# One more pair of k-tiles by seven products in two output projections of an encoder block

## The chip, the cores and the metric

The kernel runs on one core of one Trainium2 chip. The metric is the device time of one execution in microseconds (us). The engines of a core run side by side: PE (TensorE) multiplies matrices, DVE (VectorE) and ACT (ScalarE) work on elements, POOL (GpSimd) does little here, and SP (SyncE) issues the transfers from and to device memory. Each engine takes its instructions in a fixed order, and an instruction waits until what it reads has been written and the buffer it writes is free.

## The reference

One layer of an encoder on 256 tokens with 2048 channels, all in float32:

```python
x = x + 0.5 * swiglu(rms_norm(x, ffn1_norm), ffn1_w_gate, ffn1_w_up, ffn1_w_down)
h = rms_norm(x, mix_norm)
u, q, k, v, g, a_lr = jnp.split(h @ w_in, IN_SPLITS, axis=-1)
x = x + jnp.concatenate([pool_mixer(u, ...), gla_mixer(q, k, v, g, a_lr, ...)], axis=-1) @ w_out
x = x + mem_cross_attention(rms_norm(x, xattn_norm), rms_norm(mem, mem_norm), w_q, w_kv, w_o)
x = x + 0.5 * swiglu(rms_norm(x, ffn2_norm), ffn2_w_gate, ffn2_w_up, ffn2_w_down)
out = rms_norm(x, final_norm)
```

Two products matter below: the mixer's output product with `w_out` (2048 x 2048) and the attention's with `w_o` (2048 x 2048), which ends `mem_cross_attention`.

## The kernel before, in words

**Products in two parts.** Every operand is split into a high and a low part (`split`, `split_weights`), and a product of 128 x 128 by 128 x 512 is made of three instructions on PE: high by high, high by low weight, low by high weight (`products`, L356). ACT copies the high part of the weights (`wh`, L273), DVE subtracts it from the weights to get the low part (`wl`, L274).

**The stream.** A weight matrix comes in loads of 1 MB (two k-tiles of 128 rows by 1024 columns, buffer `raw`, three of them). The class `Stream` walks through all loads in order; it splits a load up to `AHEAD = 2` places before PE uses it, and asks for the load three places on as soon as a split is done. The buffers `wh` and `wl` are there three times. `op(f, n)` puts a piece of work n loads later into the order. `among_weights` and `in_turn` fix where such work stands between the splits on DVE and ACT.

**Seven products.** A load has two k-tiles and two halves of 512 columns, and there are two halves of 128 tokens: a 2 x 2 by 2 x 2 block product, 8 products of three instructions each, 24 on PE. For a pair of k-tiles that a block lists among its `sevens`, the block product is made of 7 products (21 instructions, function `seven`, L480) in Winograd's way. For that DVE adds blocks of the weights into a tile `T` (L457: one add of 128 x 1024, two of 128 x 512), ACT and DVE split the three raw blocks (`xh`, `xl`, 128 x 1536) and the four sums (`wh` L460, `wl` L461, 128 x 2048): `split_seven`. The left operand needs sums too, once for each pair: class `Sums`, with four adds on DVE (L418 to L430) and the splits of their results into the tile `ye` and back into the activations. `room` says how many pairs' sums share the first tile.

**A block.** `block_s` computes one half of the columns (1024) of an output: 8 loads in a given order of the pairs 0 to 7. Its plain products are summed in one pair of PSUM tiles; P1, P5, P6 and P7 of the seven-product pairs go to a second pair of tiles. PSUM has room for four such tiles. After the last pair of `sevens`, `combine` joins the parts (L547 to L552) and `merge` adds them to the residual x (L742); after the last load `join` adds the plain sums (L730).

**Output products.** `into_x` runs two blocks (column halves) of `block_s` for each output product. It fetches x from device memory for each half (`fetch_x`), and one load after a half ends it turns the new x (`fold`, L763), which takes two PSUM tiles, and computes its squares (L772) and its scaled parts (L242, L234). An object of `IntoX` holds the pairs, when their sums are made, the orders and the `sevens` of both halves. `OUTPUT` is the one for mixer and attention: pairs 0 and 4 by 7 products in both halves, in the 5th and 7th place of the first half and the 3rd and 5th of the second. Its sums are made by `OUTPUT.make_sums`, for the mixer 1 and 4 loads after the stream comes to it, for the attention 0 and 4.

**Where the left operands come from.** For the mixer, k-tiles 0 to 7 (pairs 0 to 3) come from the pool group and k-tiles 8 to 15 (pairs 4 to 7) from the four heads of the linear attention. For the attention, head h gives the pairs 2h and 2h + 1; the values of the last two heads (`values`, L1330) are computed while the first loads of `w_o` are being used.

**The order** of the instructions on each engine is made by a scheduler when the program is built, within what `among_weights` and its like fix. It moves single products of PE forward or back to fill waits that it expects.

## Time and profile before

| | us |
|---|---|
| median of three runs | 2085.72 |
| lowest and highest run | 2085.29, 2086.19 |
| span of the profiled execution, first to last instruction | 2085.1 |
| PE busy in it | 2071.5 |
| DVE busy | 1820.8 |
| ACT busy | 1137.5 |

The profile is that of one execution. Its span leaves out some 0.6 us before the first and after the last instruction that a run's time has. Its lines name the source line, the engine, the operation and the tiles (output, then what it is made from). A timeline's row gives the start and the duration in us, and in square brackets the idle time before it with what ended it. On PE a product's duration (0.39 us) is longer than the distance to the next one, because products overlap: PE's pace is read from starts. The same holds in a small way for DVE, whose rows overlap the next by some 0.09 us. In the chain of what ended last, each piece has its start, its length and the number of instructions.

The mixer's output product runs from about 914 to 1002 us, the attention's from about 1287 to 1380 us.

### The profile page before, as it was taken

The numbers are of one execution on the slowest core, as the hardware profiler recorded it, in microseconds if no ns is written. First come the engines' busy times: TensorE is split into PE (matmuls) and PEld (weight loads), VectorE is DVE, ScalarE is ACT, GpSimd is POOL, SyncE is SP. The second block draws the span as 40 slices with busy tenths as digits, with TensorE's granted clock in tenths as the row PEclk, the third lists the DMA queues.
The fourth block names the chain that finished last, engine by engine and source line by source line (L and its number), as shares of the span: only waits on it lengthen the run. The fifth ranks groups of instructions, "written<-read, shape, count | busy, mean of one in ns | idle before, by whom it ended". The sixth has DMA issues, their size and how long they took to land.

```text
span 2085.1 us, 24238 instructions
## 1 busy us (share of the span) xinstructions
PE 2071.5 (99%) x9660; PEld 1727.2 (83%) x9660; DVE 1820.8 (87%) x1670; ACT 1137.5 (55%) x1128; POOL 13.1 (1%) x41
## 2 busy tenths in 40 slices
PE   9999999999999999999999999999999999999998
PEld 7888888888888888888888888888888888888886
DVE  6999899989998677579789777879998999989997
ACT  7555455554555545455755444556554556545554
POOL 0000000000000000000000000000000000000001
PEclk9999999999999999999999999999999999999999
DMA  7656766566656755457655455666576665676664
GB/s 263 201 189 235 242 220 204 187 229 232 225 197 234 238 177 182 162 182 269 225 186 188 162 182 179 205 223 203 181 242 213 236 209 190 223 241 223 204 223 159
DMA packets 131321, 435.94 MB, mean 209 GB/s; under 512 B 9860, under 2 KB 13544, under 8 KB 130824
## 3 DMA queue, kind: packets, MB, share of 16 engines
q1 hardware_dynamic: 131176, 434.38, 61.4%
q8 instruction: 76, 1.25, 0.2%
q14 instruction: 37, 0.30, 0.0%
q10 hardware_dynamic: 32, 0.01, 0.0%
HBM read 417.58 MB, written 16.78 MB: 208 GB/s over the span
## 4 chain that ended last, share of the span: by engine, by line
PE 96%; DVE 2%; issue 1%; ACT 0%; DMA 0%; SPq 0%; DVEq 0%
PE pt L356 57%; PE pt L480 26%; PE pa L341 6%; PE pb L356 2%; PE ph L752 1%; PE pl L1291 1%; PE pv L1330 1%; PE px L763 1%; DVE wl L461 0%; DVE T L457 0%; DVE xl L274 0%; DVE wl L274 0%; DMA x<-in_x 0%; PE pp L984 0%; PE pe L356 0%
## 5 line engine op out<-in xcount | busy, mean ns | idle before, releaser
L274 DVE TENSOR_TENSOR wl<-raw,wh 128x2048 fp32r<-128x2048 f32 (+2 forms) x264 | 591.4, 2247 | 131.1 <-ACT wh L273 130.4
L356 PE MATMUL pt<-wh,xs 128*128 128x512 f32 x2128 | 681.8, 390 | 0.0
L273 ACT CAST wh<-raw 128x2048 fp32r<-128x2048 f32 (+2 forms) x264 | 495.4, 1880 | 284.4 <-PE pt L356 128.1
L356 PEld LDWEIGHTS pt<-wh,xs 128*128 128x128 f32 x2128 | 398.2, 188 | 81.7 <-ACT wh L273 0.4
L356 PE MATMUL pt<-wh,ys 128*128 128x512 f32 x1472 | 464.7, 390 | 0.0
L460 ACT CAST wh<-T 128x1024 fp32r<-128x1024 f32 x236 | 248.0, 1054 | 380.5 <-DVE T L457 370.0
L356 PE MATMUL pt<-wl,xs 128*128 128x512 f32 x1064 | 415.5, 391 | 0.0
L356 PEld LDWEIGHTS pt<-wh,ys 128*128 128x128 f32 x1472 | 275.9, 188 | 56.9
L356 PE MATMUL pt<-wl,ys 128*128 128x512 f32 x736 | 286.3, 389 | 0.0
L461 DVE TENSOR_TENSOR wl<-T,wh 128x2048 fp32r<-128x2048 f32 x118 | 269.5, 2284 | 0.7
L356 PEld LDWEIGHTS pt<-wl,xs 128*128 128x128 f32 x1064 | 199.8, 188 | 41.1
L274 DVE TENSOR_TENSOR xl<-raw,xh 128x1536 fp32r<-128x1536 f32 x118 | 206.7, 1752 | 19.2 <-ACT xh L273 19.2
L273 ACT CAST xh<-raw 128x1536 fp32r<-128x1536 f32 x118 | 174.6, 1480 | 41.4 <-PE pt L480 29.2
L457 DVE TENSOR_TENSOR T<-T,raw 128x512 f32<-128x512 f32 x236 | 162.8, 690 | 6.2
L356 PEld LDWEIGHTS pt<-wl,ys 128*128 128x128 f32 x736 | 138.2, 188 | 28.6
L457 DVE TENSOR_TENSOR T<-raw 128x1024 f32<-128x1024 f32 x118 | 143.8, 1219 | 0.5
L480 PE MATMUL pt<-wh,xs 128*128 128x512 f32 x364 | 141.8, 389 | 0.0
L480 PE MATMUL pt<-xh,xs 128*128 128x512 f32 x364 | 136.6, 391 | 0.1
L341 PE MATMUL pa<-xs,wh 128*128 128x512 f32 x384 | 135.6, 397 | 0.0
L480 PE MATMUL pt<-wh,xe 128*128 128x512 f32 x320 | 124.5, 389 | 0.0
L341 PE MATMUL pa<-xs,wl 128*128 128x256 f32 x384 | 106.8, 282 | 0.0
L341 PEld LDWEIGHTS pa<-xs,wh 128*128 128x128 f32 x384 | 71.7, 188 | 16.4 <-issue 0.3
(244 smaller groups left out, 2215.6 us busy)
## 6 DMA issues: line engine op xcount, KB each, us to landing
raw<-in_ffn_w_down SPq DMA_DIRECT2D x88, 1024.0 KB, 5.5
raw<-in_ffn_w_up SPq DMA_DIRECT2D x80, 1024.0 KB, 5.0
raw<-in_ffn_w_gate SPq DMA_DIRECT2D x77, 1024.0 KB, 5.1
raw<-in_w_in SPq DMA_DIRECT2D x32, 1024.0 KB, 5.2
raw<-in_xattn_w_kv SPq DMA_DIRECT2D x32, 1024.0 KB, 5.0
raw<-in_w_out SPq DMA_DIRECT2D x16, 1024.0 KB, 5.6
raw<-in_xattn_w_q SPq DMA_DIRECT2D x16, 1024.0 KB, 5.6
raw<-in_xattn_w_o SPq DMA_DIRECT2D x16, 1024.0 KB, 5.9
```

The costliest lines, as they stand in the source:

```text
L273: in_turn("scalar", lambda: nc.scalar.copy(hi, src))
L274: in_turn("vector", lambda: nc.vector.tensor_tensor(out=lo, in0=src, in1=f32(hi), op=ALU.subtract))
L341: nc.tensor.matmul(o, w, x, start=k == 0 and i == 0, stop=last and i == 1)
L356: nc.tensor.matmul(ps, a, w, start=first and i == 0, stop=last and i == 2)
L457: in_turn("vector", lambda: nc.vector.tensor_tensor(out=o, in0=a, in1=b, op=ALU.add))
L460: in_turn("scalar", lambda: nc.scalar.copy(th[:, c], t[:, c]))
L461: in_turn("vector", lambda: nc.vector.tensor_tensor(out=tl, in0=t, in1=f32(th), op=ALU.subtract))
L480: nc.tensor.matmul(banks[n], x, w, start=n in fresh and j == 0, stop=n in ends and j == 2)
L752: nc.tensor.transpose(v[:, i, h * P : (h + 1) * P], g[:, h, i * P : (i + 1) * P], ident)
L763: nc.tensor.transpose(v[:, j, h * P : (h + 1) * P], x[:, h, j * P : (j + 1) * P], ident)
L1291: nc.tensor.matmul(ps[:, t, :M], ys[:, 4 * h + d, a, tok], xa["K", h][:, d, b, :], start=i == 0, stop=i == 11,)
L1330: nc.tensor.matmul(ps[:, d, :S], xa["V", h][:, m, a, col], xa["PT", h][:, m, b, :], start=i == 0, stop=i == 5,)
```

## The change

`OUTPUT` gets a third pair, number 2 (k-tiles 4 and 5), in both halves and so in both output products. The orders are new: in the first half the 7-product pairs 2, 0, 4 stand in places 4, 6 and 7; in the second half in places 2, 4 and 6. The sums of pair 2 are made first: for the mixer after 1, 3 and 4 loads, for the attention after 0, 2 and 4. Their tile `ye` has room for three pairs instead of two.

```diff
-        def __init__(self, pairs, after, orders, sevens, over=True):
-            self.sums = Sums("ye", ys, pairs, over, 2)
+        def __init__(self, pairs, after, orders, sevens, over=True, room=2):
+            self.sums = Sums("ye", ys, pairs, over, room)
             self.after, self.orders, self.sevens = after, orders, sevens
...
-    OUTPUT = IntoX((0, 4), (0, 4), ((1, 2, 3, 5, 0, 6, 4, 7), (1, 2, 0, 3, 4, 5, 6, 7)),
-                   ((0, 4), (0, 4)))
+    OUTPUT = IntoX((2, 0, 4), (0, 2, 4), ((1, 3, 5, 2, 6, 0, 4, 7), (1, 2, 3, 0, 5, 4, 6, 7)),
+                   ((2, 0, 4), (2, 0, 4)), room=3)
...
-    OUTPUT.make_sums((1, 4))
+    OUTPUT.make_sums((1, 3, 4))
```

## The prediction

> **What bounds the kernel now.** I read the page first, for the shares, then the busy time in stretches of the two blocks, then the chain in order of time, then the timelines of the matrix and the vector engine there.

> ```profile
> span 2085.1 us, 24238 instructions
> PE 2071.5 (99%) x9660; PEld 1727.2 (83%) x9660; DVE 1820.8 (87%) x1670; ACT 1137.5 (55%) x1128; POOL 13.1 (1%) x41
> PE 96%; DVE 2%; issue 1%; ACT 0%; DMA 0%; SPq 0%; DVEq 0%
> ```

> The matrix engine (PE) is busy throughout and is 96% of the chain that ends last. That says that a removed product is a gain, as long as nothing else is short. The vector engine (DVE), busy 87% over the whole span, is not 87% busy everywhere:

> ```profile
> core 0: us, PE busy (x) PEld busy (x) DVE busy (x) ACT busy (x) POOL busy (x), PEclk, DMA share, GB/s
> 936.40:958.40 22.00, 22.00 (x99) 18.22 (x98) 20.72 (x21) 11.69 (x10) 0.00 (x0) 1.00 0.67 223
> 958.40:980.30 21.90, 21.90 (x106) 18.39 (x105) 21.04 (x23) 13.75 (x22) 0.00 (x0) 1.00 0.78 261
> 980.30:1002.00 21.70, 21.70 (x97) 17.98 (x96) 17.83 (x12) 9.28 (x6) 0.00 (x0) 1.00 0.86 317
> 1314.90:1336.70 21.80, 21.80 (x98) 18.06 (x97) 20.68 (x21) 11.70 (x10) 0.00 (x0) 1.00 0.66 220
> 1336.70:1358.70 22.00, 22.00 (x107) 18.42 (x106) 21.13 (x23) 13.76 (x22) 0.00 (x0) 1.00 0.82 266
> ```

> These are the middle of the mixer's output product (936 to 980) and of the attention's (1315 to 1359). DVE idles 1.28 + 0.86 = 2.1 us in the first 44 us and 1.12 + 0.87 = 2.0 in the second. PE and DVE are balanced there, and the change adds work to DVE in just these blocks.

> **What it removes.** The pitch of a product comes from the chain in order of time (start, us, what):

> ```profile
> 969.43 1.75 PE px L763 x16
> 977.08 5.44 PE pt L480 x24
> 984.79 22.00 PE pt L356 x97
> ```

> 5.44 / 24 = 22.00 / 97 = 0.227 us. A load of the usual kind (call its place in a block "plain") takes 24 products, one with 7 products takes 21. One more pair in each of the four output blocks (two column halves, mixer and attention) removes 4 x 3 x 0.227 = 2.7 us. This is the whole gain that is to be had: 0.13%.

> **What it adds.** The vector engine's timeline in the mixer's block shows a plain load, a pair's sums and a 7-product load one after the other without idle time:

> ```profile
> 935.01 2.29 DVE L274 TENSOR_TENSOR wl<-raw,wh 128x2048 fp32r<-128x2048 f32 x1
> 937.22 0.68 DVE L418 TENSOR_TENSOR j<-ys 128x512 f32<-128x512 f32 x1
> ...
> 939.33 1.22 DVE L457 TENSOR_TENSOR T<-raw 128x1024 f32<-128x1024 f32 x1
> 940.47 0.55 DVE L280 TENSOR_TENSOR ye<-j,ye 128x384 fp32r<-128x384 f32 x1
> 940.93 1.41 DVE L457 TENSOR_TENSOR T<-T,raw 128x512 f32<-128x512 f32 x2
> 942.26 1.75 DVE L274 TENSOR_TENSOR xl<-raw,xh 128x1536 fp32r<-128x1536 f32 x1
> 943.93 2.28 DVE L461 TENSOR_TENSOR wl<-T,wh 128x2048 fp32r<-128x2048 f32 x1
> 946.13 2.28 DVE L274 TENSOR_TENSOR wl<-raw,wh 128x2048 fp32r<-128x2048 f32 x1
> ```

> By the starts: plain 2.20 us; 7 products 1.14 + 1.33 + 1.67 + 2.20 = 6.34; sums 2.11 + 0.46 = 2.57. So each block gets 6.34 - 2.20 = 4.14 us, and mixer and attention each one more set of sums: 4 x 4.14 + 2 x 2.57 = 21.7 us of DVE time. **Bounds:** all of it hidden gives 2085.1 - 2.7 on the span; all of it exposed gives 2085.1 + 19.0. A program of this kernel takes 0.6 us more than its span (median 2085.72 beside 2085.1), so 2083.0 to 2104.7.

> How much is exposed I work out by laying the changed order of DVE instructions, which the built kernel shows, end to end with these durations, and comparing with when PE comes to the weights. First block of the mixer: 7 products now stand in places 4, 6 and 7 of 8 (before: 5 and 7).

> ```profile
> 927.60 0.69 DVE L280 TENSOR_TENSOR ys<-t,ys 128x512 fp32r<-128x512 f32 x1 [0.74 <-ACT ys L279]
> ```

> ```profile
> 947.49 0.39 PE L480 MATMUL pt<-xl,ys 128*128 128x512 f32 x1
> ```

> Before, the xl of place 7 was ready at 943.93 and PE used it at 947.49: 3.56 us to spare. Now DVE reaches it later by 4.14 + 2.57, less about 0.6 of the idle 0.74 us above, which the new order closes: 6.1 us. PE comes 3 x 0.227 = 0.7 us earlier. **PE waits 6.1 + 0.7 - 3.6 = 3.2 us** at place 7, plus some 0.1 for wl right behind it. Behind the waiting product stand all later ones: PE works in order.

> From there DVE and PE start level, and the second block begins. Its 7-product places move from 3 and 5 to 2, 4 and 6, and the merging of the first block's parts still lies in between:

> ```profile
> 952.51 1.23 DVE L549 TENSOR_TENSOR sg<-pt,sg 128x1024 f32<-128x1024 f32 x1
> ...
> 957.07 0.69 DVE L552 TENSOR_TENSOR sg<-pt,sg 128x512 f32<-128x512 f32 x1
> 957.67 1.22 DVE L742 SCALAR_TENSOR_TENSOR x<-sg,x 128x1024 f32<-128x1024 f32 x1
> ...
> 960.54 1.22 DVE L730 SCALAR_TENSOR_TENSOR x<-pt,x 128x1024 f32<-128x1024 f32 x1
> ```

> Up to the wl of place 3, DVE has to do: wl of places 7 and 8 and of place 1 (3 x 2.20), one 7-product load (6.34), L548 and L552 (0.60 each, like the 957.07 to 957.67 above), L549 (1.2), two L742 (1.13 each, a row's 1.22 less the 0.09 by which it overlaps the next) and one more wl: 19.8 us. PE has 18 + 23 + 35 = 76 products to that point, 17.2 us. **It waits about 2.5 us.** From there to the wl of place 5: DVE T (1.14), two L730 (2.26), the rest of the load (5.20), wl (2.20) = 10.8, and 0.3 for a copy of ACT's that now stands behind its squares; PE 33 products and the 16 transposes, 7.5 + 1.75 = 9.2. **It waits about 1.8 us.** After place 6 DVE's slack of 980 to 1002 (3.9 us) takes over. Mixer: 3.3 + 2.5 + 1.8 and some 0.2 of hand-over = 7.8 us.

> Attention: the same orders, but its first 7-product load stands behind the values of the last two heads.

> ```profile
> 1307.45 0.59 ACT L279 CAST ys<-pv 128x512 fp32r<-128x512 f32 x1 [0.85 <-PE pv L1330]
> 1307.93 1.48 ACT L273 CAST xh<-raw 128x1536 fp32r<-128x1536 f32 x1
> 1309.32 2.00 ACT L460 CAST wh<-T 128x1024 fp32r<-128x1024 f32 x2
> ```

> ```profile
> 1307.41 7.51 PE pt L356 x33
> 1314.92 2.72 PE pt L480 x12
> ```

> PE reaches place 4 some 5.44 us before 1314.8, at 1309.3; the values end earlier too, at about 1304.8 by the changed order, so ACT's xh copy follows at 1305.3 and xl starts at 1306.7: in time. Then DVE: wl of place 4 ends at 1310.9, then sums 2.11, wl 2.20, a 7-product load with ye 6.80, sums 2.11, and T, ye and xl of place 7, 4.6: 1328.7. PE is there after 70 products, at 1325.2: 3.5 us. With the second block as above, 8.2 us.

> **Sum:** 7.8 + 8.2 - 2.7 = +13.3 us on the span of 2085.1, with the 0.6 around it **2099.0 us**, between the bounds and nearer to full exposure, because the idle time of DVE in these stretches is 2 us each.

> Hidden: ACT's extra copies (1.48 + 2.00 in the rows above against 1.9 in the row under (c), sums 0.8) fall on an engine that is busy 11.7 of 22 us; uncovered they would be 1.6 us per block. SP fetches x for the first block one load earlier; place 7's load is issued behind it.

> ```profile
> raw<-in_w_out SPq DMA_DIRECT2D x16, 1024.0 KB, 5.6
> ```

> It lands 5.6 us after its buffer is free (about 930), and DVE asks for it at 945; without that lead the wait would be a part of 5.6 us once per product.

> **Rivals.** (a) *DVE catches up.* Only the first blocks' waits are seen, 3.3 + 3.5 - 2.7 = +4.1 us: 2089.8. For it: DVE has idle time later. Against: that lies behind place 6, and the merges stand before it. (b) *Not slower: the lead is there.* The place is the wait for ACT ahead of the block:

> ```profile
> 911.08 2.29 DVE L274 TENSOR_TENSOR wl<-raw,wh 128x2048 fp32r<-128x2048 f32 x1 [3.31 <-ACT wh L273]
> ```

> If DVE could use these 3.3 us, place 7 would be in time; from a lead of 7 us more on, all is hidden and 2083.0 remains. Against: the wait is for buffers that PE frees, and no added instruction stands ahead of it. (c) *Held buffers.* In the second block the parts of places 2 and 4 are put off to after place 5, so their high weights keep two of three buffers, and places 3, 5 and 6 share one. A copy then starts only when PE leaves the place before:

> ```profile
> 977.12 1.92 ACT L273 CAST wh<-raw 128x2048 fp32r<-128x2048 f32 x1 [0.86 <-PE pt L356]
> ```

> Copy and subtraction take 1.9 + 2.2 = 4.1 us; 9 products and 16 transposes (3.8) cover the first, 24 put-off products (5.4) the second. I count nothing; where they add to DVE's delay, up to 4.1 per second block: 2107.2. (d) *The clock.* A wait of 3.2 us is longer than PE's longest so far:

> ```profile
> 10.21 0.63 PE L689 MATMUL px<-ident,x 128*128 128x128 f32 x4 [2.21 <-DMA x<-in_x]
> 10.00:12.00 2.00, 1.79 (x10) 1.61 (x11) 0.48 (x1) 0.57 (x2) 0.00 (x0) 1.00 1.05 411
> ```

> After 2.21 us the granted clock stayed at 1.00. If it fell to half after each wait at place 7, for as long as the wait, that would cost 2 x 1.6 = 3.2 us: 2102.2. [...]

> **How the numbers follow.** Forecast 0.66 (its own range 2094 to 2104); (a) 0.15; (b) 0.04; (c) 0.07; (d) 0.08. Left out at most 2 in 10: 2088.5 to 2104.5. What this kernel's measurement can tell from no change is about 0.2%, 4.2 us: faster is out of reach of the 2.7 us (0.01); the same holds for (b) and half of (a) (0.11); slower 0.88.

> **What would show it.** PE idle with DVE's xl (L274) as releaser at the seventh place of both first blocks, about 3 us; with wl at places 3 and 5 of the second blocks, 1.5 to 3 us; DVE without gaps from 925 to 990; L480 with 84 products more, L356 with 96 fewer. Wrong it is if PE has no gaps there, if ACT or a load is the releaser, or if the granted clock drops.

## The result and the profile after

The changed kernel takes 2099.49 us (median of 4 runs, 2098.82 to 2099.82), the one before 2085.95 beside it (4 runs, 2085.29 to 2088.73): a ratio of 1.0064, 95% interval 1.0052 to 1.0076, or 13.5 us more. The forecast was 2099.0.

From the page of the changed kernel, the lines of the span, of the engines and of the chain that ended last:

```profile
span 2096.7 us, 24269 instructions
PE 2076.0 (99%) x9648; PEld 1727.0 (82%) x9648; DVE 1841.0 (88%) x1700; ACT 1144.7 (55%) x1140; POOL 13.1 (1%) x41
PE 91%; DVE 6%; issue 2%; ACT 1%; DVEq 0%; POOL 0%; ACTq 0%; POOLq 0%
```

PE has its 12 products fewer and DVE 20.2 us more. In the chain DVE's share rises from 2% to 6%. The busy times of the stretches from before show where (columns as there):

```profile
core 0: us, PE busy (x) PEld busy (x) DVE busy (x) ACT busy (x) POOL busy (x), PEclk, DMA share, GB/s
936.40:958.40 22.00, 19.39 (x77) 15.13 (x77) 21.79 (x23) 12.37 (x12) 0.00 (x0) 0.92 0.51 169
958.40:980.30 21.90, 20.18 (x95) 15.95 (x94) 21.61 (x17) 13.85 (x22) 0.00 (x0) 1.00 0.82 279
980.30:1002.00 21.70, 21.70 (x97) 17.96 (x96) 17.48 (x19) 9.61 (x7) 0.00 (x0) 1.00 0.78 277
```

DVE, with 1.3 and 0.9 us of idle time in the first two stretches before, has 0.2 and 0.3 left, and PE, which had none, idles 2.6 and 1.7 us. In the third stretch PE is full again. In the list of PE's waits (what waited, for what: us in total, times, longest) these are new; the longest of the kind L480 for xl was 0.2 us before:

```profile
PE pt L356 <- DVE wl L274: 4.0, 5, 1.2
PE pt L480 <- DVE xl L274: 3.9, 3, 1.8
PE pt L480 <- ACT wh L460: 1.5, 2, 0.8
```

PE's timeline in the mixer's block has the place of each. The first two rows are the seventh place of the first half, the others places 3 and 5 of the second:

```profile
945.87 0.50 PE L480 MATMUL pt<-wh,ye 128*128 128x512 f32 x1 [0.78 <-ACT wh L460]
948.21 0.50 PE L480 MATMUL pt<-xl,ys 128*128 128x512 f32 x1 [1.83 <-DVE xl L274]
...
967.82 0.50 PE L356 MATMUL pt<-wl,ys 128*128 128x512 f32 x1 [0.47 <-DVE wl L274]
...
978.97 0.50 PE L356 MATMUL pt<-wl,ys 128*128 128x512 f32 x1 [1.22 <-DVE wl L274]
```

The first names ACT, but ACT is not the cause. Its timeline at that place:

```profile
944.77 1.05 ACT L460 CAST wh<-T 128x1024 fp32r<-128x1024 f32 x1 [0.28 <-DVE T L457]
946.51 1.04 ACT L460 CAST wh<-T 128x1024 fp32r<-128x1024 f32 x1 [0.69 <-DVE T L457]
```

ACT itself waits for DVE's sums T. So each of PE's new waits comes from DVE.

What a wait costs is more than its bracket: I take the distance from the start of the product before, less the usual 0.227. By the starts around these four rows that is 0.95 + 2.11, 0.63 and 1.39 us, and another 0.24 at a product just ahead of the last. The clock did something too:

```profile
core 0: us, PE busy (x) PEld busy (x) DVE busy (x) ACT busy (x) POOL busy (x), PEclk, DMA share, GB/s
945.96:949.38 3.42, 1.59 (x6) 1.09 (x7) 3.42 (x3) 2.87 (x3) 0.00 (x0) 1.00 0.07 7
949.38:952.79 3.41, 3.41 (x10) 2.65 (x9) 3.41 (x3) 1.78 (x1) 0.00 (x0) 0.50 0.81 286
```

Right behind place 7 PE has half the clock (0.50) for 3.41 us, products 0.427 us apart; the same in the attention from 1335.08 on. That is some 1.7 us lost in each of the two output products. Yet it doesn't add to the 13.5 us, as the experiments show.

The block as a whole, from the start of its first product on `ys` to the start of its last:

| | mixer, from and to | length | attention, from and to | length |
|---|---|---|---|---|
| before | 914.60, 1000.49 | 85.89 | 1287.19, 1378.87 | 91.68 |
| changed | 912.85, 1004.95 | 92.10 | 1291.66, 1390.35 | 98.69 |

The mixer grows by 6.2 us and the attention by 7.0. Between the two lie 286.71 us (before 286.70), and from the attention's last product to the end of the span 706.35 (706.23). So the 13.2 us lie in these two blocks. The spans of the two profiles differ by only 11.6 us, because the mixer's block starts 1.75 us earlier in that of the changed kernel; this is taken up under "Around the span" below.

### The profile page after: what moved, and what is told of

It is laid out like the page before. It is cut to its first block, busy times and chain, and to the rows that moved or that the text cites. A ratio compares the mean times of both kernels' runs of the same rounds, so it can differ in the third digit from the quotient of the medians.

```text
span 2096.7 us, 24269 instructions
## 1 busy us (share of the span) xinstructions
PE 2076.0 (99%) x9648; PEld 1727.0 (82%) x9648; DVE 1841.0 (88%) x1700; ACT 1144.7 (55%) x1140; POOL 13.1 (1%) x41
## 4 chain that ended last, share of the span: by engine, by line
PE 91%; DVE 6%; issue 2%; ACT 1%; DVEq 0%; POOL 0%; ACTq 0%; POOLq 0%
PE pt L356 53%; PE pt L480 25%; PE pa L341 6%; PE pb L356 2%; PE ph L752 1%; DVE wl L461 1%; DVE T L457 1%; DVE wl L274 1%; DVE xl L274 1%; PE pl L1291 1%; PE pv L1330 1%; PE px L763 0%; PE pp L984 0%; PE pe L356 0%; DVE x L730 0%
## 5 line engine op out<-in xcount | busy, mean ns | idle before, releaser
L274 DVE TENSOR_TENSOR wl<-raw,wh 128x2048 fp32r<-128x2048 f32 (+2 forms) x260 | 582.1, 2247 | 122.2 <-ACT wh L273 121.6
L356 PE MATMUL pt<-wh,xs 128*128 128x512 f32 x2128 | 682.0, 390 | 0.0
L273 ACT CAST wh<-raw 128x2048 fp32r<-128x2048 f32 (+2 forms) x260 | 487.1, 1879 | 257.8 <-PE pt L356 109.9
L356 PEld LDWEIGHTS pt<-wh,xs 128*128 128x128 f32 x2128 | 398.6, 188 | 81.6 <-ACT wh L273 0.2
L460 ACT CAST wh<-T 128x1024 fp32r<-128x1024 f32 x244 | 256.3, 1053 | 382.7 <-DVE T L457 376.8
L356 PE MATMUL pt<-wh,ys 128*128 128x512 f32 x1408 | 446.7, 390 | 0.0
L356 PE MATMUL pt<-wl,xs 128*128 128x512 f32 x1064 | 415.8, 391 | 0.0
L356 PEld LDWEIGHTS pt<-wh,ys 128*128 128x128 f32 x1408 | 264.1, 188 | 54.8 <-ACT wh L273 0.4
L461 DVE TENSOR_TENSOR wl<-T,wh 128x2048 fp32r<-128x2048 f32 x122 | 278.8, 2285 | 1.5 <-ACT wh L460 0.5
L356 PE MATMUL pt<-wl,ys 128*128 128x512 f32 x704 | 274.5, 390 | 4.0 <-DVE wl L274 4.0
L274 DVE TENSOR_TENSOR xl<-raw,xh 128x1536 fp32r<-128x1536 f32 x122 | 213.7, 1752 | 23.2 <-ACT xh L273 23.2
L356 PEld LDWEIGHTS pt<-wl,xs 128*128 128x128 f32 x1064 | 199.9, 188 | 41.2
L273 ACT CAST xh<-raw 128x1536 fp32r<-128x1536 f32 x122 | 180.5, 1480 | 59.5 <-PE pt L480 40.0
L457 DVE TENSOR_TENSOR T<-T,raw 128x512 f32<-128x512 f32 x244 | 168.5, 691 | 6.3
L356 PEld LDWEIGHTS pt<-wl,ys 128*128 128x128 f32 x704 | 132.2, 188 | 33.3 <-DVE wl L274 6.2
L457 DVE TENSOR_TENSOR T<-raw 128x1024 f32<-128x1024 f32 x122 | 148.8, 1220 | 0.5
L480 PE MATMUL pt<-wh,xs 128*128 128x512 f32 x364 | 141.8, 389 | 0.0
L480 PE MATMUL pt<-xh,xs 128*128 128x512 f32 x364 | 136.5, 391 | 0.1
L480 PE MATMUL pt<-wh,xe 128*128 128x512 f32 x320 | 124.5, 389 | 0.0
## 6 DMA issues: line engine op xcount, KB each, us to landing
raw<-in_ffn_w_down SPq DMA_DIRECT2D x88, 1024.0 KB, 5.6
raw<-in_ffn_w_up SPq DMA_DIRECT2D x80, 1024.0 KB, 5.0
raw<-in_ffn_w_gate SPq DMA_DIRECT2D x77, 1024.0 KB, 5.1
raw<-in_w_in SPq DMA_DIRECT2D x32, 1024.0 KB, 5.2
raw<-in_xattn_w_kv SPq DMA_DIRECT2D x32, 1024.0 KB, 5.0
raw<-in_w_out SPq DMA_DIRECT2D x16, 1024.0 KB, 5.5
raw<-in_xattn_w_q SPq DMA_DIRECT2D x16, 1024.0 KB, 5.6
raw<-in_xattn_w_o SPq DMA_DIRECT2D x16, 1024.0 KB, 5.6
```

The source lines that it names most:

```text
L273: in_turn("scalar", lambda: nc.scalar.copy(hi, src))
L274: in_turn("vector", lambda: nc.vector.tensor_tensor(out=lo, in0=src, in1=f32(hi), op=ALU.subtract))
L356: nc.tensor.matmul(ps, a, w, start=first and i == 0, stop=last and i == 2)
L457: in_turn("vector", lambda: nc.vector.tensor_tensor(out=o, in0=a, in1=b, op=ALU.add))
L460: in_turn("scalar", lambda: nc.scalar.copy(th[:, c], t[:, c]))
L461: in_turn("vector", lambda: nc.vector.tensor_tensor(out=tl, in0=t, in1=f32(th), op=ALU.subtract))
```

## The experiments

Theory: *DVE is late.* PE loses the time by which DVE's added work exceeds DVE's lead and idle time. Rivals: the new *orders* with their held buffers cost by themselves; the half *clock* makes the loss or a part of it. Each diff is against the changed kernel. `into_x` takes another object by `way=`, `TWO` has the values of `OUTPUT` before. Where a diff adds lines, the line numbers of the trace are shifted by a few. Times are set against the runs of the kernel before on the same chip (2085.68, 2085.50 and 2085.71 us in three groups of runs).

**mix_only**

```diff
+    TWO = IntoX((0, 4), (0, 4), ((1, 2, 3, 5, 0, 6, 4, 7), (1, 2, 0, 3, 4, 5, 6, 7)),
+                ((0, 4), (0, 4)))
...
-    OUTPUT.make_sums()
-    into_x(w_o, ys, 1.0, G_FFN2, spread_too=False)
+    TWO.make_sums()
+    into_x(w_o, ys, 1.0, G_FFN2, spread_too=False, way=TWO)
```

> The third pair only in the mixer's output product; the attention's keeps the orders and the two pairs of the kernel before. Late vector engine (the forecast's theory): the two blocks share nothing, so the loss is about half of the whole change's 13.5 us, 6.7 us above the kernel before, and the mixer's gaps of the matrix engine are those of the changed kernel (1.8 us with xl, about 0.6, 0.2 and 1.2 us with wl or ACT's wh), none at the attention's place 7. If the attention's waits hang on a time that the mixer passes on, this kernel loses 10 us or more and the attention's part alone under 4.

**att_only**: the same for `w_out`, with `TWO.make_sums((1, 4))`.

> The third pair only in the attention's output product; the mixer's is that of the kernel before. Late vector engine: about 6.8 us above the kernel before, the sum with the mixer's part 13.5 within 1 us. Granted clock: one stretch of about 3.4 us at half, behind the attention's place 7, none in the mixer. If the two parts interact, the sum of the two kernels' losses differs from 13.5 by more than 2 us.

Measured: 2092.37 us, +6.7 (ratio 1.0031, 1.0020 to 1.0043) and 2092.03, +6.4 (1.0032, 1.0019 to 1.0044). Together 13.0 of the 13.5 us: the blocks share nothing. The unchanged block of each is as long as before (91.68 and 85.89 us), and each has one stretch at half clock, behind its own place 7.

**orders_only**

```diff
-    OUTPUT = IntoX((2, 0, 4), (0, 2, 4), ((1, 3, 5, 2, 6, 0, 4, 7), (1, 2, 3, 0, 5, 4, 6, 7)),
-                   ((2, 0, 4), (2, 0, 4)), room=3)
+    OUTPUT = IntoX((0, 4), (2, 4), ((1, 3, 5, 2, 6, 0, 4, 7), (1, 2, 3, 0, 5, 4, 6, 7)),
+                   ((0, 4), (0, 4)))
-    OUTPUT.make_sums((1, 3, 4))
+    OUTPUT.make_sums((3, 4))
```

> The changed orders of the k-tiles, but only the two pairs of before with 7 products, so the vector engine's work is that of before. Late vector engine: the work is what counts, not the order: within 1.5 us of the kernel before, no gap of the matrix engine over 0.5 us in the two blocks. Rival, orders and held weight buffers: the put-off loads of places 2 and 4 keep their buffers here too, as does the copy of x behind them, so 3 us or more of the loss of 13.5 are seen, in the second halves.

**orders_early**: as orders_only, but the sums at `(0, 4)` and `make_sums((1, 4))`, as before the change.

> The changed orders of the k-tiles with the two pairs of before, as in orders_only, but the two sums at the places that they have in the kernel before (in the attention 0 and 4 loads, in the mixer 1 and 4, in place of 2, 4 and 3, 4). If the 5.0 us of orders_only are the place of the sums, which puts the values of the last heads behind a weight subtraction that waits for its buffer, they go: within 1 us of the kernel before, by products_only (-2.0) plus its 2.7 about +0.7, and no wait of the matrix engine for ys. If they are the order of the k-tiles, 4 us or more stay.

Measured: orders_only 2090.70, +5.0 (1.0025, 1.0015 to 1.0035), a miss of my theory's 1.5 us, and it would have spoken for the orders. But its waits stand elsewhere than in the changed kernel, around the third place of the attention's first half. (The profile is that of the fastest run, 2088.24 us: the attention's block is 3.6 us longer than before, the mixer's is not.) PE's list of waits, then DVE's timeline there:

```profile
PE pv L1330 <- DVE ys L280: 2.0, 1, 2.0
...
PE pt L356 <- ACT ys L279: 1.0, 1, 1.0
```

```profile
1294.81 0.68 DVE L418 TENSOR_TENSOR j<-ys 128x512 f32<-128x512 f32 x1
...
1298.57 2.29 DVE L274 TENSOR_TENSOR wl<-raw,wh 128x2048 fp32r<-128x2048 f32 x1 [1.56 <-ACT wh L273]
1300.78 1.22 DVE L457 TENSOR_TENSOR T<-raw 128x1024 f32<-128x1024 f32 x1
1301.92 0.55 DVE L280 TENSOR_TENSOR ye<-j,ye 128x384 fp32r<-128x384 f32 x1
1302.39 1.28 DVE L280 TENSOR_TENSOR ys<-pv,ys 128x512 fp32r<-128x512 f32 x2
```

The values of two heads (`ys<-pv`) stand behind a subtraction that waits 1.56 us for ACT's copy, and behind T. From the third place on, the block multiplies these values. With the sums earlier, orders_early takes 2085.91, +0.2 (1.0002, 0.9993 to 1.0011), and its mixer's block is 85.89 us long. So the new orders by themselves cost nothing; a misplaced sum costs some 5 us with no added work. The changed kernel has no wait at that place. With pair 2 plain, orders_early doesn't have all of the held buffers; the next kernel has them.

**products_only**

```diff
-    OUTPUT = IntoX((2, 0, 4), (0, 2, 4), ((1, 3, 5, 2, 6, 0, 4, 7), (1, 2, 3, 0, 5, 4, 6, 7)),
-                   ((2, 0, 4), (2, 0, 4)), room=3)
+    OUTPUT = IntoX((0, 4), (0, 4), ((1, 3, 5, 2, 6, 0, 4, 7), (1, 2, 3, 0, 5, 4, 6, 7)),
+                   ((2, 0, 4), (2, 0, 4)))
-    OUTPUT.make_sums((1, 3, 4))
+    OUTPUT.make_sums((1, 4))
+            g = g if g in self.pairs else self.pairs[0]
             i, n = self.pairs.index(g), 3 if self.over else 4
...
-            def fn(weights):
+            def fn(weights, low=None):
+                if low is not None:
+                    h, l = (w.rearrange("p (b n) -> p b n", n=NB) for w in (weights, low))
+                    weights = (h, l, h[:, 1:], l[:, 1:])
...
-                st.unit(srcs[g], unit_s(g), split_seven)
+                st.unit(srcs[g], unit_s(g), split_seven if g in sums.pairs else None)
```

> The changed orders and all of the changed kernel's products, but the third pair's weights come from a plain split and its sums are those of the first pair: the three additions of weights in four loads and two sets of sums are left out, and the output is not the reference's. Late vector engine: the gain shows alone, 12 products x 0.227 = 2.7 us below the kernel before (1.5 to 3.0), no clock at half. Rival, a sequence of 21 products or another order costs the matrix engine by itself: no gain, or slower than before.

Measured: 2083.69, 2.0 us below the kernel before (0.9990, 0.9982 to 0.9999), and 2.2 below orders_early. The gain is real, though the interval only just leaves out no change: in the profile each of the two blocks is 1.0 us shorter than before, for 1.36 by the sum. The held buffers are here too: in the mixer's second half, PE makes the 24 products that are put off, together with the 21 of place 6, from 977.19 on. ACT waits for PE there, 2.71 us before a copy of weights at 982.15, but the list of PE's waits has none in either block. So the held buffers cost nothing by themselves.

**no_sums**: as products_only without the last two edits, so that the third pair keeps its `split_seven`.

> The changed kernel with the third pair's weights split as for 7 products, but without that pair's own sums: it takes those of the first pair (left out: 2.57 us of the vector engine in each product; the output is not the reference's). Late vector engine: place 7 of the first halves waits 2.6 us less than the changed kernel's 0.8 + 1.8 us, so next to nothing; the second halves start with that lead only in part. About 5 us less in all than the changed kernel, 8 to 9 us above the kernel before. Granted clock: without the 2.6 us there is no stretch at half, and if such stretches cost their 1.7 us on top of everything, this kernel falls to about 5 us above; if they only take the place of later waits for the vector engine, the waits of the second halves are longer here than in the changed kernel by about 1.7 us.

Measured: 2093.82, +8.3 (1.0040, 1.0025 to 1.0054), as expected. The mixer's place 7 loses 0.7 us, the attention's still 1.4; at place 3 of the mixer's second half stand 2.1 us, and at place 5 1.4. I had expected no half clock; there is one in the attention, from 1350.25 on, behind a place 3 of 2.1 us. There the loss of 1.4 at place 5 is gone. That was the first sign that the half clock takes the place of a wait.

**first_half** and **second_half** give the third pair only one half: the other half has the order and the pairs 0 and 4 of before. Since a pair's sums are written over a part of its activations, the half that multiplies pair 2 in the plain way reads that part overwritten; the work is the same.

```diff
-    ... (1, 2, 3, 0, 5, 4, 6, 7)), ((2, 0, 4), (2, 0, 4)), room=3)
+    ... (1, 2, 0, 3, 4, 5, 6, 7)), ((2, 0, 4), (0, 4)), room=3)
```

> The third pair only in the first column halves; the second halves have the order and the two pairs of before. Late vector engine: the first halves' waits stay (about 0.9 + 2.1 us at place 7, the half clock behind them), minus 6 products x 0.227 = 1.4 us: 3.0 + 1.7 - 0.7 = 4.0 us per product at most, 8 us in all, if the second halves then have no wait; with the half clock eating up what would be a wait 5 us. Rival, the loss comes from the second halves' held buffers: under 3 us.

```diff
-    ... ((1, 3, 5, 2, 6, 0, 4, 7), (1, 2, 3, 0, 5, 4, 6, 7)), ((2, 0, 4), (2, 0, 4)), room=3)
+    ... ((1, 2, 3, 5, 0, 6, 4, 7), (1, 2, 3, 0, 5, 4, 6, 7)), ((0, 4), (2, 0, 4)), room=3)
```

> The third pair only in the second column halves; the first halves have the order and the two pairs of before, and the sums are still made in the first halves. Late vector engine: 4.14 + 2.57 us of added work before place 5 of the second halves, less the lead of 3.6 us there was at place 7, less a little idle time: waits of 2 to 3.5 us in the second halves, minus 0.7 us of products: +4 us in all (2 to 6), spread over places 1 to 5, so no stretch at half clock. With first_half the two make up more than the changed kernel's 13.5 less 2 only if no lead is shared.

Measured: first_half 2094.32, +8.8 (1.0042, 1.0029 to 1.0055; 2092.24 to 2096.55, a wide spread), second_half 2090.09, +4.6 (1.0023, 1.0013 to 1.0032): together 13.4, which is near 13.5 in part by chance, as the profiles show. In first_half's profile, that of the fastest run, the waits at place 7 are there to a hundredth (0.77 and 1.83 us), the second halves have none in the mixer and 0.34 us in the attention, and the clock doesn't fall in the blocks: these grow by 2.8 and 4.2 us. The two longest runs, 2094.64 and 2096.55 us, have the lowest granted clocks, 0.997 and 0.996 beside 0.998 in the others. With hardly a wait behind it to take the place of, a half clock may add here; no profile of these runs shows it. Against the rival of 3 us, most of the loss is the first halves' sums and splits. In second_half the size came out and the place only in part: of its second halves only place 5 has a wait, 1.14 us in the mixer and 1.24 in the attention. And 1.94 us, one wait at place 2 of the mixer's first half, come from the experiment itself: there PE reads the overwritten part of pair 2, which DVE writes (`ys<-j`, L280, 924.11) behind a subtraction of weights. The changed kernel has no such wait.

**four_loads**

```diff
-    OUTPUT = IntoX((2, 0, 4), (0, 2, 4), ((1, 3, 5, 2, 6, 0, 4, 7), (1, 2, 3, 0, 5, 4, 6, 7)),
-                   ((2, 0, 4), (2, 0, 4)), room=3)
+    OUTPUT = IntoX((2, 0, 4), (0, 2, 4), ((1, 3, 5, 2, 0, 6, 4, 7), (1, 2, 3, 0, 5, 4, 6, 7)),
+                   ((2, 0, 6, 4), (2, 0, 4, 6)), room=3)
...
+            g = g if g in self.pairs else self.pairs[0]
             i, n = self.pairs.index(g), 3 if self.over else 4
```

> The changed kernel with a fourth pair of k-tiles (the last but one load of each half) split for 7 products and multiplied by 7; its own sums are left out, it takes those of the first pair, and the output is not the reference's. Late vector engine: once more 4.14 us of added work per half and 0.68 us of products less. The first halves give it in full, 3.46 us each; the second halves too, less what is left of the 3.9 us of idle time behind place 6: 13.5 + 2 x 3.5 to 13.5 + 2 x 6.9 = 20.5 to 27.4 us above the kernel before. If the loss is a fixed price of the one late place, or made of the half clock, under 18.

Measured: 2114.13, +28.4 (1.0139, 1.0125 to 1.0152), twice the loss with twice the loads. It is 1 us above the upper bound, since I had let the loss end with the block. In the profile the blocks grow by 10.2 and 10.8 us, 20.9 us together beside the 20.5 to 27.4 that I had given them; another 3.2 and 3.4 us lie behind them. PE's timeline of this kernel, behind the mixer's block (its last product starts at 1009.88):

```profile
1029.43 0.73 PE L356 MATMUL pt<-wh,xs 128*128 128x512 f32 x2 [1.04 <-ACT wh L273]
1031.76 0.50 PE L356 MATMUL pt<-wl,xs 128*128 128x512 f32 x1 [1.59 <-DVE wl L274]
```

The next stage, which reads `xs`, waits for weights too; in the changed kernel it has no such wait. That the idle time behind place 6 is used up would explain it, but isn't shown: DVE stands idle for ACT for 3.06 us just ahead, at 1022.29.

**pool_adds**

```diff
-            in_turn("vector", lambda: nc.vector.tensor_tensor(out=o, in0=a, in1=b, op=ALU.add))
+            in_turn(engine, lambda: adds.tensor_tensor(out=o, in0=a, in1=b, op=ALU.add))
...
```

Here `engine` and `adds` are POOL in the four blocks of `OUTPUT`, and the 128 x 1024 addition is two of 128 x 512.

> The changed kernel, but the three additions of weights of each load with 7 products in these four blocks run on POOL (four 128x512 additions) in place of the vector engine: 6.34 - 2.20 = 4.1 us of a load with 7 products leave the vector engine but for its longer start, some 10 us per half. Late vector engine: with that the waits go, and the gain is left: 2 to 3 us below the kernel before, if POOL's additions come in time (four of 1.5 us at best in 10 us). Rival, POOL is too slow, or the two engines hold each other up: waits for T with POOL as releaser or longer rows of the vector engine, and the time stays above the kernel before.

Measured: 2117.36, +31.9 (1.0153, 1.0139 to 1.0167). The rival is right, in both its parts: ACT's copies of the sums wait 20.4 us for POOL in the two products, and DVE's rows become longer. POOL's group, then two rows of DVE beside a busy POOL and one beside an idle POOL:

```profile
L460 POOL TENSOR_TENSOR T<-raw 128x512 f32<-128x512 f32 x24 | 48.7, 2049 | 494.3 <-PE pv L1336 321.4 <-DVE j L430 125.6 <-DVE wl L464 21.0
```

```profile
938.30 1.27 DVE L425 TENSOR_TENSOR j<-j 128x128 f32<-128x128 f32 x1
939.60 1.33 DVE L426 TENSOR_TENSOR j<-j 128x128 f32<-128x128 f32 x1
...
951.29 0.29 DVE L426 TENSOR_TENSOR j<-j 128x128 f32<-128x128 f32 x1
```

POOL's addition takes 2.05 us on average in this group. From 923.8 to 947.6 POOL is adding, but for 2.06 us before 931.92, and from there to 959.7 it is idle: the same DVE operation takes 1.33 us in the first stretch and 0.29 in the second. So work moved to POOL isn't simply off DVE here. By what DVE is held up, these rows don't show.

**again1** and **again2**: the changed kernel, unchanged.

> The changed kernel once more, for the phase of the clock. The waits at place 7 of the first halves are the same (about 0.8 + 1.8 us with one product between). If the clock is set from a fixed grid of 3.41 us, a stretch at half follows only where 2 us or more of the idle time lie in one window of it; with 1.8 us or less in each of two there is none, and then the waits for the vector engine in the second half behind it are longer by 1.4 to 1.7 us, so that the block ends within 0.5 us of where it ended. If the half clock adds to the loss, a product without it is 1.7 us shorter.

> The changed kernel a third time, another phase of the clock's grid; the same theories and numbers as for again1, the more of the four stretches behind place 7 without half clock the better they are told apart.

Measured: again2 fell to half clock at both places, again1 at neither (one run each, 2099.41 and 2102.23 us). The 2 us of idle time in one window that I had taken to be needed are too many: the changed kernel's windows that lose the clock have 1.83, as the last section shows. PE's timeline of again1 in the mixer, to be held against the four rows of the changed kernel above:

```profile
949.24 0.50 PE L480 MATMUL pt<-wh,ye 128*128 128x512 f32 x1 [0.79 <-ACT wh L460]
951.57 0.49 PE L480 MATMUL pt<-xl,ys 128*128 128x512 f32 x1 [1.83 <-DVE xl L274]
...
971.27 0.50 PE L356 MATMUL pt<-wl,ys 128*128 128x512 f32 x1 [1.91 <-DVE wl L274]
...
982.42 0.50 PE L356 MATMUL pt<-wl,ys 128*128 128x512 f32 x1 [1.24 <-DVE wl L274]
```

The third is 1.91 us in place of 0.47: without the half clock PE comes earlier and waits longer. The block runs from 916.22 to 1008.43, 92.21 us beside 92.10, in the attention from 1295.14 to 1393.76, 98.62 beside 98.69. The half clock costs nothing here, since DVE sets the time behind it. Again1 is longer as a whole for what lies at its start: the 2.2 us wait for x that the profile of before has too, and a stretch at half clock behind it, with which its mixer's block starts 1.62 us later than that of before (916.22 beside 914.60).

## Why the prediction was right, step by step

| step (us) | forecast | changed | again1 |
|---|---|---|---|
| mixer, place 7 of the first half | 3.3 | 0.95 + 2.11 | 0.95 + 2.11 |
| half clock behind it | 0 | 1.7 | 0 |
| place 3 of the second half | 2.5 | 0.63 | 2.07 |
| place 5 | 1.8 | 0.24 + 1.39 | 0.24 + 1.40 |
| 6 products fewer | -1.36 | -1.36 | -1.36 |
| the block | +6.4 | +6.2 | +6.3 |
| attention, the block | +6.8 | +7.0 | +6.9 |

- **The gain**, 2.7 us: products_only has 2.0 of it.
- **The added work**, 21.7 us by starts: the page has 20.2 us more of busy time. The third set of sums alone is worth 13.5 - 8.3 = 5.2 us (no_sums), twice its 2.57.
- **Place 7**: 3.06 us for 3.3, at the place and with the releaser named. It came in two pieces, the first by way of ACT's `wh`, which waits for T.
- **Second halves**: 3.7 us of waits in again1 for 4.3. The terms were each a little long; what was entered as 0.2 us of hand-over makes this good. By the table, 6.32 + 1.36 - 3.06 - 2.07 - 1.64 = 0.9 us lie in pauses too short to be listed.
- **Attention**: place 7 is 0.9 + 2.1 for 3.5, and place 5, at which the prediction names no wait, loses 0.75 us before it: 3.75 in all. The prediction's own rows have that wait: the weights of place 5 ready at 1310.9 + 2.11 + 2.20 = 1315.2, PE there after 22 products, at 1314.3. A wait taken at place 5 is missing at place 7, so the sum held. (Its 1310.9 is 0.3 us late by the same rows: 1306.7 + 1.67 + 2.20 = 1310.6.)
- **Hidden**: ACT's copies and the fetch of x cost nothing, as said. No transfer is among PE's waits in the blocks.
- **Rivals.** (a) fell by the second halves' waits. (b) fell: DVE stands the same 3.31 us for `wh` ahead of the block (at 909.32 now), and place 7 is late. A longer lead would take a fourth buffer of weights; it wasn't tried. (c) fell by products_only, with the orders themselves cleared by orders_early. Its wait exists on DVE, 1.98 us for `xh` at 986.49, but PE is busy throughout that stretch (21.70 of 21.70). (d) had the fall right and the price wrong. The clock did fall, to 0.50 for 3.41 us behind place 7 in each block, which the prediction called a sign against itself. I had 1.00 behind the 2.21 us wait of the profile before and nothing on a longer one, and added 3.2 us if it fell, an estimate. Half clock ahead of a wait for a late engine is a wait that PE spends working: nothing is added here, 92.10 us for the mixer's block with it and 92.21 in again1 without.
- **Around the span**: mis-sized. I took 0.6 us from the median beside the span of another execution. The runs of again1 and again2, each timed and profiled in one, have 2102.23 - 2100.1 and 2099.41 - 2097.3 = 2.1 us; in the runs of the kernel before beside the experiments it is some 1.8. By luck, that was made up for by the 2.2 us wait for x at the start, which the profile of before has (the span of 2085.1 on which I built) and that of the changed kernel has not: 2085.1 + 13.2 - 1.8 (the block starts 914.60 - 912.85 earlier) = 2096.5, beside 2096.7. So the 0.5 us between the forecast and the measured time are closer than the prediction earned; the difference of 13.3 us, for which 13.5 were measured, doesn't rest on this luck.

No version here that does all of the work beats the kernel before: products_only bounds what 7 products for this pair could bring at 2 us, and DVE has 20 us of work for it.

## What to carry to other kernels

Before work is moved from a full engine to another, compare the two amounts in the stretch where they fall: here 0.68 us of PE were bought with 4.14 us of DVE, which had 1 us idle in 22. Lay the other engine's new order end to end from its rows, and the wait comes out to some tenths of a us, with its place. And look at where auxiliary work is queued: the same sums, two loads later in the order, cost some 5 us, because values needed at once stood behind a subtraction that had to wait itself.

## What the runs showed of the hardware

```profile
core 0: us, PE busy (x) PEld busy (x) DVE busy (x) ACT busy (x) POOL busy (x), PEclk, DMA share, GB/s
946.42:949.83 3.41, 2.53 (x10) 1.39 (x8) 3.34 (x7) 2.48 (x3) 0.00 (x0) 1.00 0.26 106
949.83:953.25 3.42, 1.68 (x7) 1.42 (x8) 3.42 (x3) 3.37 (x3) 0.00 (x0) 1.00 0.24 28
953.25:956.66 3.41, 3.41 (x16) 2.55 (x14) 3.41 (x3) 1.29 (x1) 0.00 (x0) 1.00 0.74 279
```

The wait is the same, but the grid cuts it in two, and with 1.68 us the clock stays at 1.00. So it does with 1.74 in first_half, while behind again2's 1.01 it is 0.50. The windows ahead of a fall aren't idle as a whole: in these traces up to 1.59 of 3.41 us busy (with modelled ends) were enough to fall and 1.68 were not, so whether the clock fell behind the same 2.6 us of wait, as in the changed kernel, or not, as in again1, was a matter of phase. One window does not fit: at the end of again2, from 2086.07 on, 1.49 us are busy, nothing behind them, and the next window still has the full clock; so the border is not sharp by this measure. For the way back even 2.81 us were not enough: in four_loads a window at half clock with 2.81 us busy (from 1329.93 on) is followed by another at half, in pool_adds one with 3.24 us (from 946.33 on) by full clock, as the changed kernel's two with 3.41 us are.
